# The first modulation as small products on TensorE, with products of ones around them, and the Fourier branch split into even and odd tokens

## The chip, the cores and the metric

The kernel runs on one core of a Trainium2 chip. The metric is the device time of one execution in microseconds (us). A core has a matrix engine (TensorE, PE in the profile; its weight loads are listed apart as PEld), three other compute engines (VectorE or DVE, ScalarE or ACT, GpSimd or POOL) and a queue that issues the transfers from memory (SyncE or SP). Each engine works through its own list in order and waits on the others by semaphores.

## The reference

Two layers of a transformer over 256 latent and 256 context tokens of 1024 features. Only what the change touches is shown in full.

```python
m = silu(cond) @ w_mod + b_mod                     # 9 x 1024 values a layer, for latent and context each
u = rms_norm(x, g) * (1 + scale) + shift           # shift, scale: parts 0 and 1 of m for the first sublayer
x = x + 0.5 * gate * (silu(u @ Wa) * (u @ Wb)) @ Wout        # first FFN, 2816 wide
...
# token mixing: attention beside a Fourier branch of 4 groups of 128 channels
f = u @ w_four_in                                  # 512 channels
y = Re(fft2(f.reshape(S, 4, 128), axes=(tokens, channels), norm="ortho"))
merged = sigmoid(ga) * a + sigmoid(gf) * (y @ w_four_out)
...
# second FFN; in layer 1 the context stream is dropped after its keys and values; final RMS norm
```

## The kernel before, in words

Features lie on the 128 partitions; the 512 tokens (256 latent, then 256 context) lie along the free dimension, so `x` is 8 chunks of 128 features by 512 tokens. Every large product is done in three: operands are split into a high part (fp32r) and the remainder, and `mm3` (L369) adds high x high, high x low and low x high (L373, L374, L375). Weights come as blocks of 128 x 1024 through the class `Stream`: `load_to` (L165) issues the transfer, `split_pieces` (L172) makes `whi` on ACT (L184) and `wlo` on DVE or POOL (L185), `next` hands a block out and keeps some loads and splits ahead. The order on each engine is the order in which the Python program issues instructions; all waits come from data and from buffers (46 slots of 4 KB a partition, 7 temporaries, 8 PSUM banks of 128 x 512).

**The start (L1095 to L1198).** The first FFN needs `u`, and `u` needs shift and scale, 16 chunks of 128 values for each of the two conditions. Before, each chunk is a dot product on DVE: `mod_dot` (L299, instruction L302) multiplies a 128 x 1024 block of `w_mod` by the condition, which `cond_spread` has put on all partitions, and sums along the row. For each of the 8 feature chunks `j` the loop at L1157 issues two dots for latent and two for context, the scaled `x` (L1132, on POOL or DVE), two small affines on ACT (L1143, L1145), shift and scale on ACT (L1149), the high part (L1150) and the low part on POOL or DVE (L1154). Meanwhile `ffn` (L597) works on the first `START_PAIRS` = 4 column pairs of the FFN at once: 8 PSUM banks, and for each `k` the products of `u[k]` with 8 weight chunks, latent and context apart (256 columns each). These are the rows `pf`. The other 18 pairs follow one by one, over 512 columns (rows `pa` and `pb`, 48 products a pair). From then on the remaining modulation dots (L302) are dealt out two to a weight block (`tick`), beside the products.

**The Fourier branch (L706 to L755).** It lies at the end of the attention, in heads' steps 8, 9 and 10 and in front of the first merged column. The lists `STEPS` and `TAIL` (L56, L61) give the order of the named steps within a head's turn. For each of 4 groups: `fourier_project` makes 128 channels by all tokens (rows `pfc`); `fourier_channels` multiplies each 128 tokens by a 128 x 256 table of cosines and sines over channels (rows `pch`), and splits the result (`ab`, ACT and DVE); `fourier_positions` multiplies by the 256 x 256 tables over tokens (rows `pseq`). `y` is used by the products `pfo` in the merge (L1068). In layer 1 only the latent tokens go through it.

Of the kernel before, what the change touches and what calls it, by code (L numbers as in the profile page):

```python
# [18 lines left out]
P = 128  # L19
# [21 lines left out]
START_PAIRS = 4  # L41
# [85 lines left out]

def constants():
# [14 lines left out]
    rope = np.stack([cos * scale, sin * scale, cos, sin], axis=1).astype(np.float32)  # L143
# [4 lines left out]
    b = 2 * np.pi * ((s[:, None] * s[None, :]) % S) / S  # L148
    sq = np.stack([np.cos(b), -np.sin(b)]) / math.sqrt(S)
    sq = sq.reshape(2, 2, P, S).transpose(2, 1, 0, 3)  # L150
    return rope.reshape(P, 4 * S), ch.astype(np.float32), np.ascontiguousarray(sq.astype(np.float32)).reshape(P, 4 * S)
# [60 lines left out]
def tile_kernel(ctx: ExitStack, tc, d, out):  # L212
# [45 lines left out]

    def cond_load():
        for n in range(2):  # L260
            cond["row", n] = slot.tile([P, D], F32, tag="s", name="crow")
            nc.sync.dma_start(cond["row", n][:1], d["cond"][n:n + 1, :])

    def cond_spread():

        for n in range(2):
            row = cond.pop(("row", n))
            cond[n] = slot.tile([P, D], F32, tag="s", name="cond")
            for h in range(2):
                hc = slice(h * 512, (h + 1) * 512)  # L270
                ps = bank("pcond")
                nc.tensor.matmul(ps, ones[:1, :], row[:1, hc], start=True, stop=True)
                nc.scalar.activation(cond[n][:, hc], ps, AF.Silu)

    nc.gpsimd.memset(ones, 1.0)
    nc.gpsimd.memset(eps, EPS)
    cond_load()
    nc.sync.dma_start(x[:, :, :S], d["x"][:, :, :S])

# [9 lines left out]
    mod_n = [0, 0, 0]  # L289
# [307 lines left out]
    def ffn(l, f, ss, u, later, after):  # L597
# [8 lines left out]
        if l == 0 and f == 1:  # L606
            for n in range(2):
                cond[n] = slot.tile([P, D], F32, tag="s", name="cond")
                nc.sync.dma_start(cond[n], d["cond"][n:n + 1, :].partition_broadcast(P).rearrange("p a b -> p (a b)"))
# [28 lines left out]
        for n, part in enumerate(stagger):  # L638
            c = cols(part)
            ps = [bank("pf") for _ in range(2 * first)]  # L640
            for k in range(KC):
                if n == 0 and (k * 2 * first) % 8 == 0:
                    w.extend(st.tiles(8))
                for sub in [[s] for s in part] if first == START_PAIRS else [part]:
                    cs = slice(0, S + 2) if e else cols(sub)
                    for q in range(2 * first):
                        mm3(ps[q][:, cs], w[k * 2 * first + q], parts(e.v[k] if e else u[k], cs), k == 0 and sub[0] == part[0], k == KC - 1 and sub[-1] == part[-1])
# [28 lines left out]
    def mixing(l, ss, u, later, after):  # L676
# [31 lines left out]
        def fourier_load():  # L708
            dft["raw"] = slot.tile([P, 1024], F32, tag="s", name="ft"), temp("ft2")
            nc.sync.dma_start(dft["raw"][0], d["dft_sq"])  # L710
            nc.sync.dma_start(dft["raw"][1][:, :256], d["dft_ch"])

        def fourier_tables():

            sq, ch = dft.pop("raw")
            dft["sq"] = [slot.tile([P, 1024], F32R, tag="s", name="dft") for _ in range(2)]
            nc.scalar.activation(dft["sq"][0], sq, AF.Copy)
            nc.gpsimd.tensor_tensor(out=dft["sq"][1], in0=sq, in1=dft["sq"][0].bitcast(F32), op=ALU.subtract)
            dft["ch"] = hilo("dch")
            split(dft["ch"], slice(0, 256), ch[:, :256])  # L720

        fo = {}

        def fourier_project(g):
            tiles = st.tiles(8)
            c = cols(ss)
            ps = bank("pfc")
            for k in range(KC):
                mm3(ps[:, c], tiles[k], parts(u[k], c), k == 0, k == KC - 1)
            fo["f", g] = hilo("f")  # L730
            split(fo["f", g], c, ps[:, c])

        def fourier_channels(g):
            f = fo.pop(("f", g))
            for s in ss:
                ps = bank("pch")
                for t in range(2):
                    fc = slice(s * S + t * P, s * S + (t + 1) * P)
                    q = slice(t * 256, (t + 1) * 256)
                    mm3(ps[:, q], parts(f, fc), parts(dft["ch"], slice(0, 256)), True, True)  # L740
                ab = fo[s, g] = hilo("ab")
                split(ab, slice(0, 512), ps)

        def fourier_positions(g):
            ps = bank("pseq")
            for s in ss:
                ab = fo.pop((s, g))
                for n in range(4):
                    t, cs = divmod(n, 2)
                    q = slice(t * 256 + cs * P, t * 256 + (cs + 1) * P)  # L750
                    rhs = slice(n * S, (n + 1) * S)
                    mm3(ps[:, cols([s])], parts(ab, q), (dft["sq"][0][:, rhs], dft["sq"][1][:, rhs]), n == 0, n == 3)
            c = cols(ss)
# [251 lines left out]
        def fourier(h):  # L1005
            if h == NH:
                fourier_tables()
            if h >= NH:
                fourier_project(h - NH)
# [251 lines left out]
```

## Time and profile before

| | |
|---|---|
| median of 3 runs (lowest, highest) | 2031.62 us (2031.35, 2031.69) |
| the profiled execution, whole | 2031.67 us |
| its span, first to last instruction | 2029.9 us |
| PE, DVE, ACT, POOL busy, share of the span | 98%, 61%, 41%, 40% |
| mean granted TensorE clock | 0.999 of full speed |
| read from memory | 286.91 MB |

A busy share counts an instruction from its start to its end, and products on PE overlap, so the pace of PE is read from the distance between the starts of neighbouring products, not from their durations. "Idle before <- releaser" is the time an engine stood still before a group, and what ended it. The time of the profiled execution lies 1.8 us above its span.

### The profile page before, as it was taken

What the parts mean: (1) busy time and instruction counts of PE and PEld (TensorE: products, weight loads), DVE (VectorE), ACT (ScalarE), POOL (GpSimd) and SP (SyncE); (2) the same over time, 40 slices, a digit from 0 to 9 for tenths busy, and PEclk for the clock granted to TensorE, in tenths of its full rate; (3) what the DMA queues carried; (4) which work ended last, traced back from release to release, by engine and by line L of the source; (5) the groups of instructions that cost most, each with busy time, mean ns of one, the idle gap of its engine ahead of it and who ended that gap; (6) DMA issues with size and microseconds to landing.
All of it is one profiled execution on the core that took longest, in us unless ns stands there. A gap on an engine that the chain in (4) does not pass through costs nothing.

```text
span 2029.9 us, 27251 instructions
## 1 busy us (share of the span) xinstructions
PE 1992.1 (98%) x10476; PEld 1710.7 (84%) x10476; DVE 1244.3 (61%) x1819; ACT 839.2 (41%) x1383; POOL 804.0 (40%) x531
## 2 busy tenths in 40 slices
PE   7899999999999999999999999999999999999998
PEld 5788888888888888988888898888888889998887
DVE  8887787657777234677777543323324687667662
ACT  5532232256666234522322233223323566656661
POOL 7653446445544012244348511111221454214463
PEclk9999999999999999999999999999999999999999
DMA  9355565523332333455559532222421334555461
GB/s 374 119 177 177 177 219 195 168 66 94 105 96 89 94 106 128 149 178 176 157 196 348 181 125 83 83 83 84 129 89 63 116 123 136 170 187 180 154 217 63
DMA packets 86534, 297.08 MB, mean 146 GB/s; under 512 B 9858, under 2 KB 13314, under 8 KB 86404
## 3 DMA queue, kind: packets, MB, share of 16 engines
q1 hardware_dynamic: 86116, 294.82, 43.3%
q8 instruction: 82, 1.34, 0.3%
q10 hardware_dynamic: 288, 0.52, 0.1%
q14 instruction: 48, 0.39, 0.1%
HBM read 286.91 MB, written 1.05 MB: 142 GB/s over the span
## 4 chain that ended last, share of the span: by engine, by line
PE 89%; DVE 4%; DMA 2%; issue 2%; ACT 1%; POOL 1%; SPq 0%; DVEq 0%; POOLq 0%; ACTq 0%
PE po L374 7%; PE po L373 7%; PE po L375 7%; PE pb L375 5%; PE pb L374 5%; PE pb L373 5%; PE pa L374 5%; PE pa L375 5%; PE pa L373 5%; PE pg L374 2%; PE pg L375 2%; PE pg L373 2%; PE po L380 2%; PE pb L380 2%; PE pa L380 2%
## 5 line engine op out<-in xcount | busy, mean ns | idle before, releaser
L185 POOL TENSOR_TENSOR wlo<-wraw,whi 128x1024 fp32r<-128x1024 f32 (+1 forms) x154 | 394.0, 2560 | 555.0 <-ACT whi L184 461.8
L184 ACT ACTIVATE whi<-wraw 128x1024 fp32r<-128x1024 f32 (+1 forms) x400 | 397.3, 1032 | 73.3 <-PE po L374 33.9
L185 DVE TENSOR_TENSOR wlo<-wraw,whi 128x1024 fp32r<-128x1024 f32 x246 | 340.4, 1394 | 115.8 <-ACT whi L184 114.3
L302 DVE SCALAR_TENSOR_TENSOR junk<-mraw,cond 128x1024 bf16<-128x1024 f32 x256 | 363.3, 1463 | 0.3
L373 PE MATMUL po<-g,whi 128*128 128x512 f32 (+1 forms) x616 | 223.8, 363 | 0.0
L374 PE MATMUL po<-g,whi 128*128 128x512 f32 (+1 forms) x616 | 223.3, 362 | 0.0
L375 PE MATMUL po<-g,wlo 128*128 128x512 f32 (+1 forms) x616 | 223.3, 362 | 0.0
L317 POOL TENSOR_SCALAR mval<-macc,small 128x2 f32<-128x2 f32 (+1 forms) x88 | 122.4, 1396 | 212.3 <-DVE junk L302 212.1
L629 ACT ACTIVATE g<-gv 128x512 fp32r<-128x512 f32 (+1 forms) x92 | 51.7, 562 | 371.0 <-DVE gv L628 339.1
L375 PE MATMUL pb<-u,wlo 128*128 128x512 f32 x464 | 180.6, 389 | 0.6 <-POOL wlo L185 0.6
L375 PE MATMUL pa<-u,wlo 128*128 128x512 f32 x464 | 180.6, 389 | 0.3 <-POOL wlo L185 0.3
L373 PE MATMUL pa<-u,whi 128*128 128x512 f32 x464 | 180.7, 389 | 0.0
L374 PE MATMUL pa<-u,whi 128*128 128x512 f32 x464 | 180.6, 389 | 0.0
L374 PE MATMUL pb<-u,whi 128*128 128x512 f32 x464 | 180.5, 389 | 0.0
L373 PE MATMUL pb<-u,whi 128*128 128x512 f32 x464 | 180.5, 389 | 0.0
L628 DVE TENSOR_TENSOR gv<-silu,pb 128x512 f32<-128x512 f32 x58 | 39.9, 688 | 182.4 <-PE pb L375 181.6
L462 DVE SCALAR_TENSOR_TENSOR x<-po,mval,x 128x256 f32<-128x256 f32 x73 | 32.7, 479 | 186.8 <-PE po L375 186.8
L373 PEld LDWEIGHTS po<-g,whi 128*128 128x128 f32 x616 | 116.2, 189 | 18.3
L375 PEld LDWEIGHTS po<-g,wlo 128*128 128x128 f32 x616 | 116.2, 189 | 18.1
L374 PEld LDWEIGHTS po<-g,whi 128*128 128x128 f32 x616 | 116.2, 189 | 18.1
L424 POOL TENSOR_TENSOR acc<-acc,sq 128x256 f32<-128x256 f32 (+1 forms) x46 | 54.1, 1175 | 184.2 <-ACT sq L413 184.1
L413 ACT ACTIVATE sq<-x 128x256 f32<-128x256 f32 (+1 forms) x48 | 24.8, 516 | 233.7 <-DVE x L462 203.0
(261 smaller groups left out, 4700.5 us busy)
## 6 DMA issues: line engine op xcount, KB each, us to landing
wraw<-in_ffn_in SPq DMA_DIRECT2D x176, 512.0 KB, 4.2
mraw<-in_w_mod SPq DMA_DIRECT2D x144, 512.0 KB, 3.8
wraw<-in_ffn_out SPq DMA_DIRECT2D x88, 512.0 KB, 4.4
wraw<-in_qk SPq DMA_DIRECT2D x32, 512.0 KB, 3.8
wraw<-in_g SPq DMA_DIRECT2D x32, 512.0 KB, 3.7
wraw<-in_v SPq DMA_DIRECT2D x16, 512.0 KB, 3.7
wraw<-in_attn SPq DMA_DIRECT2D x16, 512.0 KB, 3.5
wraw<-in_wo SPq DMA_DIRECT2D x16, 512.0 KB, 3.6
```

What stands on the lines that cost most here:

```text
L184: nc.scalar.activation(hi[:, c], raw[:, c], AF.Copy)
L185: eng.tensor_tensor(out=lo[:, c], in0=raw[:, c], in1=hi[:, c].bitcast(F32), op=ALU.subtract)
L302: nc.vector.scalar_tensor_tensor(out=tmp.tile([P, D], BF16, tag="t", name="junk"), in0=mod_raw[n], scalar=1.0, in1=cond[s], op0=ALU.mult, ...
L317: eng.tensor_scalar(out=o, in0=v, scalar1=b_mod[:, b:b + 1], scalar2=0.5 if i % 3 == 2 else 1.0, op0=ALU.add, op1=ALU.mult)
L373: nc.tensor.matmul(ps, hi, uh, start=first, stop=False)
L374: nc.tensor.matmul(ps, hi, ul, start=False, stop=False)
L375: nc.tensor.matmul(ps, lo, uh, start=False, stop=last)
L380: nc.tensor.matmul(ps.rearrange("p (a b) -> p a b", a=2), hi, t[:, :, c], start=first, stop=False)
L424: nc.gpsimd.tensor_tensor(out=self.acc[:, c], in0=self.acc[:, c], in1=sq[:, c], op=ALU.add)
L462: nc.vector.scalar_tensor_tensor(out=x[:, m, c], in0=ps[:, c], scalar=mod(l, 3 * i + 2, m, s), in1=x[:, m, c], op0=ALU.mult, op1=ALU.add)
L628: nc.vector.tensor_tensor(out=v[:, c], in0=sl[:, c], in1=pb[:, c], op=ALU.mult)
L629: nc.scalar.activation(g[j][:, 0, c], v[:, c], AF.Copy)
```

## The change

**Start.** The two condition vectors also come transposed (`cond_t`, 128 x 16). `silu` of them is written into a zeroed tile of 8 chunks by 32 columns (`cond_w`, 2 columns used). The first 2048 columns of `w_mod` come untransposed, 1 MB for each `j`. `first_mod(j)` issues 8 plain fp32 products of 256 columns with 32 stationary columns each; product `k` writes the partitions 32t to 32t + 31 of one bank, t = k mod 4, so four strips are summed apart. DVE copies them out, and `first_sum(j)` adds the four strips and turns the result onto the partitions with two fp32 products of 2 columns against `pick`; two small operations on DVE finish shift and scale. `first_u` makes `u` with two DVE operations and one ACT operation per stream. `START_PAIRS` goes from 4 to 3, so 6 banks are held by `pf`; a new function `start` writes the order out by hand: for `k` = 0 and 1 latent and context apart, for `k` = 2 to 7 both at once over 512 columns, with `first_sum(k+1)` after the first 6 products of `k` and `first_mod(k+2)` after the last 12. `busy` issues fp32 products of ones with ones, 128 columns each: 24 at the very start, 6 and 4 later. The spread conditions (`cond`, for the later dots) are loaded last in the start and their `silu` is done on ACT at `k` = 5. The norm's sum of squares is folded to two products a stream.

**Fourier.** Tokens are renumbered on the host, even ones first, then odd ones (rope tables and output too). `fourier_project` now has tokens as the stationary side and the 512 channels along the free dimension, one bank for each 128 tokens. The position step comes first: for a group and a stream, 128 even tokens and 128 odd tokens are each multiplied by one 128 x 256 table (128 positions, cosine and sine); ACT copies the odd half out, DVE adds and subtracts to get positions 0 to 127 and 128 to 255, and the result is split. Two groups are done at once. The channel step is last and makes `y` over all tokens at once. Loads, table splits and the places in the head steps change accordingly.

PE's list from its first product, before:

```order
L272 MATMUL pcond<-crow,ones 128x512 x4
L1121 MATMUL ss<-sq,ones 128x256 x8
L373 MATMUL pf<-u_148,whi 128x256
L374 MATMUL pf<-u_148,whi 128x256
L375 MATMUL pf<-u_148,wlo 128x256
```

and the same place now (`pwarm` and the second `pf` row are products of ones, `pmod` the modulation, `msb` its copy):

```order
L1142 MATMUL pwarm<-ones 128x128 x24
L1183 MATMUL pmod<-mfirst,cond_w 32x256 x8
L1172 MATMUL ss<-sq,ones 128x256 x2
L1193 MATMUL pmod<-pick,msb 128x2 x2
L1142 MATMUL pf<-ones 128x128 x6
L373 MATMUL pf<-u_180,whi 128x256
L374 MATMUL pf<-u_180,whi 128x256
L375 MATMUL pf<-u_180,wlo 128x256
```

The modulation and the norm now stand on PE in front of the first `pf`; the eight sums of squares have become two for the stream that is needed first.

DVE's list in the start, before (from the first dots on; `junk` is the written-out product of a dot, `macc` its sum):

```order
L302 SCALAR_TENSOR_TENSOR junk,macc<-mraw,cond 128x1024 x2
L1132 TENSOR_TENSOR ut<-x,rinv 128x256
L302 SCALAR_TENSOR_TENSOR junk,macc<-mraw,cond 128x1024
L1154 TENSOR_TENSOR u_148<-ut,u_148 128x256
L302 SCALAR_TENSOR_TENSOR junk,macc<-mraw,cond 128x1024
L1132 TENSOR_TENSOR ut<-x,rinv 128x256
L302 SCALAR_TENSOR_TENSOR junk,macc<-mraw,cond 128x1024 x2
```

and now, one turn of `start` (`k` = 3 to 4):

```order
L1200 TENSOR_SCALAR mval<-pmod,small 128x2
L1200 TENSOR_SCALAR mval<-pmod,bm_80,small 128x2
L1207 SCALAR_TENSOR_TENSOR ut<-x,mval,rinv 128x256 x2
L1211 SCALAR_TENSOR_TENSOR u_183<-ut,mval,u_183 128x256 x2
L1185 COPY msb<-pmod 128x256
```

The dots are gone from DVE here; a turn has a copy, two small operations and four of 256 columns, and in some turns the low part of a weight block.

DVE's list at the end of layer 1's heads, before (`f` is the split projection, `ab` the split channel step, `orinv` the norm of a head's output):

```order
L395 TENSOR_TENSOR f_14526<-pfc_14501,f_14526 128x256
L395 TENSOR_TENSOR ab_14536<-pch_14529,ab_14536 128x512
L944 SCALAR_TENSOR_TENSOR orinv_14541<-pav_14464,sub_g_79,orinv_14541 128x256
L395 TENSOR_TENSOR ao_14560<-orinv_14541,ao_14560 128x256
L185 TENSOR_TENSOR wlo_14564<-wraw_14434,whi_14563 128x1024
L395 TENSOR_TENSOR f_14594<-pfc_14569,f_14594 128x256
L395 TENSOR_TENSOR ab_14604<-pch_14597,ab_14604 128x512
```

and now:

```order
L395 TENSOR_TENSOR f_14353<-pfc_14258,f_14353 128x512
L395 TENSOR_TENSOR f_14356<-pfc_14262,f_14356 128x512
L962 SCALAR_TENSOR_TENSOR orinv_14361<-pav_14290,sub_g_79,orinv_14361 128x256
L395 TENSOR_TENSOR ao_14380<-orinv_14361,ao_14380 128x256
L193 TENSOR_TENSOR wlo_14388<-wraw_14325,whi_14387 128x1024
L756 TENSOR_TENSOR ab_14409<-pseq_14391,odd_14398 128x4x64
L757 TENSOR_TENSOR ab_14409<-pseq_14391,odd_14398 128x4x64
L756 TENSOR_TENSOR ab_14412<-pseq_14400,odd_14407 128x4x64
L757 TENSOR_TENSOR ab_14412<-pseq_14400,odd_14407 128x4x64
L764 TENSOR_TENSOR ab_14416<-ab_14409,ab_14415 128x512
L764 TENSOR_TENSOR ab_14419<-ab_14412,ab_14418 128x512
```

Both halves of the tokens are now projected and split before the position step, which has two additions or subtractions a group.

The diff, cut to its core:

```diff
-START_PAIRS = 4
+START_PAIRS = 3
+WARM = 24
+TOKENS = np.arange(S).reshape(P, 2).T.reshape(-1)
...
-    mod_n = [0, 0, 0]
+    mod_n = [2 * KC, 2 * KC, 0]
...
+            if first == START_PAIRS:
+                ps = start(first, w, u)
...
-        def fourier_project(g):
-            tiles = st.tiles(8)
-            ps = bank("pfc")
-            for k in range(KC):
-                mm3(ps[:, c], tiles[k], parts(u[k], c), k == 0, k == KC - 1)
...
+        def fourier_project(ns, ks):
+            for k in ks:
+                if ns[0] == 0 and k % 2 == 0:
+                    hi, lo = st.next()
+                    fw.extend([(hi[:, :512], lo[:, :512]), (hi[:, 512:], lo[:, 512:])])
+                for n in ns:
+                    if k == 0:
+                        fp[n] = bank("pfc")
+                    mm3(fp[n], parts(u[k], slice(n * P, (n + 1) * P)), fw[k], k == 0, k == KC - 1)
...
+        def fourier_positions(s, gs):
+            for g in gs:
+                ps[g] = bank("pseq")
+                for t in range(2):
+                    q = slice(t * 2 * P, (t + 1) * 2 * P)
+                    mm3(ps[g][:, q], parts(fo["f", 2 * s + t], gc), [p[:, q] for p in dft["p"]], True, True)
+                nc.scalar.activation(odd[g], ps[g][:, 2 * P:].rearrange("p (a b) -> p a b", a=4), AF.Copy)
+            for g in gs:
+                nc.vector.tensor_tensor(out=q[:, :, :P // 2], in0=even, in1=odd[g], op=ALU.add)
+                nc.vector.tensor_tensor(out=q[:, :, P // 2:], in0=even, in1=odd[g], op=ALU.subtract)
...
         def fourier_channels(g):
+            for n in range(2):
+                q = slice((4 + n) * P, (5 + n) * P)
+                mm3(ps[:, c], [p[:, q] for p in dft["p"]], (hi[:, n], lo[:, n]), n == 0, n == 1)
...
         def fourier(h):
+            n = h - NH
+            if n in (0, 1):
+                fourier_project((0, 1), range(n * KC // 2, (n + 1) * KC // 2))
+            if n == 2:
+                if CTX in ss:
+                    fourier_project((2,), range(KC))
+                fourier_positions(LAT, range(NG // 2))
...
+    def busy(ps, n):
+        for _ in range(n):
+            nc.tensor.matmul(ps[:, :P], ones, ones, start=True, stop=True)
+    busy(bank("pwarm"), WARM)
...
+    def first_mod(j):
+        ps = bank("pmod")
+        for k in range(KC):
+            t = k % 4
+            nc.tensor.matmul(ps[32 * t:32 * t + 32, :2 * P], cond_w[:, k, :], raw[k // 4][:, t, :], start=k < 4, stop=k >= 4)
+        nc.vector.tensor_copy(sb, ps[:, :2 * P])
+    def first_sum(j):
+        for i in range(2):
+            nc.tensor.matmul(ps[:, q:q + 2], sb[:, i * P:(i + 1) * P], pick[:, :2], start=True, stop=True)
...
+    def start(first, w, u):
+        first_mod(0)
+        first_norm(LAT, sq)
+        first_sum(0)
+        first_u(0, [LAT])
+        weights_to(0)
+        busy(ps[-1], 6)
+        sq = squares(CTX)
+        products(0, [LAT], every)
+        first_mod(1)
+        first_norm(CTX, sq, 4)
+        first_sum(1)
+        first_u(1, [LAT])
+        weights_to(1)
+        first_u(0, [CTX])
+        products(1, [LAT], every)
+        first_mod(2)
+        first_u(1, [CTX])
+        products(0, [CTX], every)
+        first_sum(2)
+        first_u(2, both)
+        weights_to(2)
+        products(1, [CTX], every)
+        first_mod(3)
+        for k in range(2, KC):
+            products(k, both, every[:2])
+            if k + 1 < KC:
+                first_sum(k + 1)
+                first_u(k + 1, both)
+                weights_to(k + 1)
+            if k == 5:
+                nc.scalar.preload_act_table_set(SILU)
+                for n in range(2):
+                    nc.scalar.activation(cond[n], cond[n], AF.Silu)
+            products(k, both, every[2:])
+            if k + 2 < KC:
+                first_mod(k + 2)
```

More of the change, by code (lines that the diff above doesn't have):

```diff
@@ L257, in tile_kernel @@
     cond = {}
+    nc.gpsimd.memset(ones, 1.0)
+    nc.gpsimd.memset(eps, EPS)
+    cond_t = slot.tile([P, KC, 2], F32, tag="s", name="cond_t")
+    nc.sync.dma_start(cond_t, d["cond_t"])
+    for n in range(2):
+        nc.sync.dma_start(x[:, 4 * n:4 * n + 4, :S], d["x"][:, 4 * n:4 * n + 4, :S])
     def cond_load():
         for n in range(2):
[L261 to L267, printed above, removed]
-            cond[n] = slot.tile([P, D], F32, tag="s", name="cond")
[L269 to L278, printed above, removed]
+            cond[n] = slot.tile([P, D], F32, tag="s", name="cond")
+            nc.sync.dma_start(cond[n], d["cond"][n:n + 1, :].partition_broadcast(P).rearrange("p a b -> p (a b)"))
     def mod_tasks():
@@ L606, in ffn @@
         if l == 0 and f == 1:
[L607 to L609 removed]
+            cond_load()
         def gated(j, pa, pb, c):
@@ L639, in ffn @@
             c = cols(part)
-            ps = [bank("pf") for _ in range(2 * first)]
-            for k in range(KC):
+            if first == START_PAIRS:
+                ps = start(first, w, u)
+            else:
+                ps = [bank("pf") for _ in range(2 * first)]
+            for k in range(KC) if first != START_PAIRS else ():
                 if n == 0 and (k * 2 * first) % 8 == 0:
                     w.extend(st.tiles(8))
[L644 to L647, printed above, removed]
+                cs = slice(0, S + 2) if e else c
+                for q in range(2 * first):
+                    mm3(ps[q][:, cs], w[k * 2 * first + q], parts(e.v[k] if e else u[k], cs), k == 0, k == KC - 1)
                 if n == 0 and k == (E_K if e else 4) and later:
@@ L733, in fourier_channels @@
-        def fourier_channels(g):
[L734 to L753, printed above, removed]
+            raw = dft.pop("raw")
@@ new lines, in squares, with first_norm @@
+        nc.scalar.activation(sqs[1], x[:, 4:, c], AF.Square)
+        nc.vector.tensor_tensor(out=sqs[0], in0=sqs[0], in1=sqs[1], op=ALU.add)
+        nc.vector.tensor_tensor(out=sqs[0][:, :2], in0=sqs[0][:, :2], in1=sqs[0][:, 2:], op=ALU.add)
+        return sqs[0]
+    def first_norm(s, sq, n=0):
+        ps = bank("ss")
+        busy(ps, n)
+        c = cols([s])
+        for m in range(2):
+            nc.tensor.matmul(ps[:, c], ones, sq[:, m, :], start=m == 0, stop=m == 1)
+        rinv[s] = rsqrt(ps, D, c, "rinv")
@@ L1236 @@
         "rope": rope,
-        "dft_ch": dft_ch,
-        "dft_sq": dft_sq,
+        "dft": dft,
     }
```

252 lines of the change are left out of this document (133 added, 119 removed).

## The prediction

> **What bounds the kernel now.** I read the page first, then the busy time by stage, then what PE waited for, then the start in order of time.
>
> ```profile
> span 2029.9 us, 27251 instructions
> PE 1992.1 (98%) x10476; PEld 1710.7 (84%) x10476; DVE 1244.3 (61%) x1819; ACT 839.2 (41%) x1383; POOL 804.0 (40%) x531
> ```
>
> By stage (columns: stretch, length, busy us of each engine, granted clock, DMA share, GB/s):
>
> ```profile
> 0.00:20.00 20.00, 14.61 (x25) 7.76 (x25) 11.73 (x12) 9.14 (x15) 8.16 (x13) 1.00 0.87 321
> 20.00:54.00 34.00, 26.12 (x192) 23.70 (x192) 34.00 (x37) 18.74 (x43) 31.24 (x20) 1.00 1.02 406
> 54.00:87.70 33.70, 25.64 (x192) 23.59 (x192) 31.18 (x40) 18.82 (x38) 30.31 (x19) 1.00 0.30 93
> 87.70:2015.00 1927.30, 1919.26 (x10023) 1649.98 (x10022) 1163.56 (x1726) 791.23 (x1285) 731.74 (x478) 1.00 0.43 141
> ```
>
> From 87.7 to 2015 us PE stands still for 8 of 1927 us, so there a product that goes away is time saved. Before 87.7 PE is not the bound: DVE is full, and transfers are full only until 54. Who PE waits for in the start, and what DVE does up to 87.7:
>
> ```profile
> PE pf L374 <- POOL u L1154: 11.4, 7, 1.6
> PE pf L375 <- POOL wlo L185: 3.7, 8, 0.8
> L302 DVE SCALAR_TENSOR_TENSOR junk<-mraw,cond 128x1024 bf16<-128x1024 f32 x32 | 62.1, 1985 | 0.1
> 87.56 0.28 PE L375 MATMUL pf<-u,wlo 128*128 128x256 f32 x1
> 87.68 0.50 PE L373 MATMUL pa<-u,whi 128*128 128x512 f32 x1
> ```
>
> The modulation dots hold DVE for 62 us; the low parts of `u` on POOL come behind them. The first `pa` at 87.7 is the mark for the start.
>
> **PE's pace.** Starts of neighbouring products in a full stretch:
>
> ```profile
> 1214.75 0.28 PE L374 MATMUL pf<-u,whi 128*128 128x256 f32 x1
> ...
> 1217.39 0.28 PE L375 MATMUL pf<-u,wlo 128*128 128x256 f32 x1
> 1217.51 0.40 PE L373 MATMUL pa<-u,whi 128*128 128x512 f32 x1
> ...
> 1221.84 0.39 PE L374 MATMUL pa<-u,whi 128*128 128x512 f32 x1
> ```
>
> 22 steps in 2.64 us: 0.120 us for 256 columns. 19 steps in 4.33 us: 0.228 us for 512.
>
> **Fourier: the sure part.** The groups of before (one of three lines each):
>
> ```profile
> L373 PE MATMUL pseq<-dft,ab 128*128 128x256 f32 x48 | 13.6, 283 | 0.0
> L373 PE MATMUL pch<-dch,f 128*128 128x256 f32 x24 | 6.8, 282 | 0.0
> L373 PE MATMUL pfc<-u,whi 128*128 128x512 f32 x32 | 13.1, 409 | 0.0
> L373 PE MATMUL pfc<-u,whi 128*128 128x256 f32 x32 | 9.3, 291 | 0.0
> ```
>
> That is 144 + 72 products of 256 for positions and channels, a third of them in layer 1. Layer 0: 144 x 0.120 = 17.3 us become 48 x 0.120 (positions) and 24 x 0.228 (channels) = 11.2: 6.1 less. Layer 1: 72 x 0.120 = 8.6 become 48 x 0.120 = 5.8: 2.9 less. Layer 1's projection: 96 x 0.120 = 11.5 becomes 48 x 0.228 = 10.9: 0.6 less; layer 0's stays at 96 of 512. Sum **9.5 us**, all on PE where PE is full. The two additions, the copy and the split of each position step need DVE and ACT, but what reads them (`pch`) stands behind at least a gate projection of 48 x 0.120 = 5.8 us (layer 1) or 24 x 0.228 = 5.5 us (layer 0). The weak spot is layer 1's last head: its sum of squares `pss` now stands behind 12 products (1.4 us) after the head's values, where there were 42.
>
> ```profile
> PE pss L942 <- ACT osq L928: 1.1, 1, 1.1
> 1745.12 0.38 ACT L928 ACTIVATE osq<-pav 128x256 f32<-128x256 f32 x1 [0.45 <-PE pav L375]
> ```
>
> With no cover at all PE waited 1.1 us at an earlier head; 1.4 us of cover is enough if ACT comes at once, as it does here. I take 0, with 2 us as the upper bound for all new waits here.
>
> **The start, by chains.** Transfers, norm and fp32 products:
>
> ```profile
> 0.00:5.00 5.00, 2.73 (x4) 1.19 (x5) 0.00 (x0) 1.88 (x2) 1.15 (x9) 1.00 0.38 111
> 5.00:10.00 5.00, 4.44 (x6) 1.30 (x4) 2.59 (x3) 1.72 (x3) 2.06 (x2) 1.00 1.04 351
> 10.00:15.00 5.00, 3.78 (x8) 2.52 (x8) 4.63 (x5) 2.41 (x3) 2.29 (x1) 1.00 1.03 410
> 11.33 1.06 ACT L1114 ACTIVATE sq<-x 128x1024 f32<-128x1024 f32 x1 [1.26 <-DMA x<-in_x]
> 16.18 3.55 PE L1121 MATMUL ss<-sq,ones 128*128 128x256 f32 x8 [1.24 <-POOL sq L1118]
> 400.66 0.59 PE L430 MATMUL ss<-acc,ones 128*128 128x256 f32 x2
> L430 PE MATMUL ss<-acc,ones x20: 377/377/380, 400.7 to 2020.4; 128*128 128x256 f32 x20
> ```
>
> Delivered by 10 us: 5 x 111 + 5 x 351 KB = 2.3 MB, then 0.41 MB/us. All of `x` (2.2 MB with what goes ahead) had landed at 11.33, when 2.85 MB were through: a load lands about 0.6 MB after its own bytes. In the new order the first modulation block ends at 2.1 MB: 2.7 MB are through at 11.0 us. The second (4.85 MB) comes at 17.7, the eighth (14.3 MB) at 41; both are asked for later, so DMA is not the bound, and the 1 MB of spread conditions behind them delays only blocks needed after 75 us.
>
> An fp32 product leaves two records. Warm, they are 0.59 - 0.377 = 0.213 us apart (0.43 a product of 256 columns); early, 3.55 / 8 = 0.444 (0.89).
>
> **The disputed price: `first_mod`, f.** No row shows products on a quarter of the columns. All four strips at once: two rounds of 0.43, f = 0.85. None beside another: 16 x 0.213 = 3.4. I take **2.1**, midway, which is also what follows if records start in order, as in every timeline here: a strip's second record waits for its first, the next strip's first runs beside it, 9 x 0.213 and one drain (0.377 - 0.213). [...] `first_sum` is four records bounded by a weight load each; 8 fp32 transposes of 128 columns ran at 0.109:
>
> ```profile
> 1715.62 0.87 PE ptr L894 x8
> ```
>
> I take 0.6 us with the small products behind the loads (0.45 to 0.9).
>
> The links on other engines:
>
> ```profile
> 15.04 0.47 ACT L400 ACTIVATE rinv<-ss,eps 128x256 f32<-128x256 f32 x1 [1.35 <-PE ss L1121]
> L446 DVE SCALAR_TENSOR_TENSOR ut<-x,mval,rinv x72: 471/479/1919, 402.2 to 1847.2; 128x256 f32<-128x256 f32 x72
> L1150 ACT ACTIVATE u<-ut x16: 416/418/420, 18.7 to 83.4; 128x256 fp32r<-128x256 f32 x16
> L809 DVE TENSOR_SCALAR rs<-rs,lam x48: 213/214/217, 456.8 to 1736.3; 128x1 f32<-128x1 f32 x48
> L184 ACT ACTIVATE whi<-wraw 128x1024 fp32r<-128x1024 f32 (+1 forms) x400 | 397.3, 1032 | 73.3 <-PE po L374 33.9
> L185 DVE TENSOR_TENSOR wlo<-wraw,whi 128x1024 fp32r<-128x1024 f32 x246 | 340.4, 1394 | 115.8 <-ACT whi L184 114.3
> ```
>
> First turn: `first_mod` 11.0 to 13.1, two norm products to 14.0, logarithm and exponential to 15.0, `first_sum` and two small operations (0.21 each) to 15.1, scaled `x` 15.6, high part 16.1, then on ACT's list the weight block's high part 17.1, on DVE its low part 18.5: the third product waits for that, and 18 x 0.120 end at 20.5. Second turn the same way: `first_mod` 22.6, four products of ones and the norm 24.3, `first_sum` 24.9, `u` 26.4, low part of the block 28.9, products end at 30.2. From here PE has its own work: 2 x 2.1 + 36 x 0.120 + 0.6 = 9.1, to 39.3. Then `k` = 2 to 7: 108 x 0.228 + 5 x 0.6 + 4 x 2.1 = 36.0, to **75.3**.
>
> Is that covered? After `first_sum` the chain to both streams' low parts is about 0.2 + 2 x 0.21 + 0.48 + 0.42 + 2 x 0.48 + hops = 2.7 us; PE has 12 x 0.228 + 2.1 = 4.8. A block split behind it (0.42 + 1.03 + 1.39 more) is just ready. The table load and two `silu` of 1024 columns on ACT at `k` = 5 (some 3.3 us in front of the last `u`) end before that `u` is asked for, by under 1 us; uncovered they cost 3. DVE has some 4 us in a turn of 6.8, so it is no longer the bound.
>
> After 75.3 there is one more pair, 48 x 0.228 = 10.9: before's point is reached at 86.2, against 87.7. **The start gains 1.5 us**; the price f decides its sign, by 8 us for each us.
>
> The clock: a cold PE at 11 us would make the first `first_mod` and norm 3 us longer. The 24 products of ones are put there for that. In this trace the one-row products went 7 us without getting faster:
>
> ```profile
> L272 PE MATMUL pcond<-crow,ones 1*128 1x512 f32 x8 | 7.2, 1072 | 2.3 <-DMA crow<-in_cond 2.3
> ```
>
> The granted clock reads 1.00 throughout and can't tell. [...]
>
> **Sum.** 2031.7 (the profiled execution, 0.05 from the median; 1.8 us of it lie outside the span and stay) - 9.5 - 1.5 = **2020.7 us**.
>
> **Rivals.**
> - *Four strips at once*, f near 1.0: 8 x 1.1 less, some 0.5 given back where PE reaches a block before its low part: 2012.4. For it: the strips share no columns. Against: two records a product, started in order. [...] Chance 0.22.
> - *The strips don't overlap*, f = 3.6 with the drain: 8 x 1.5 = 12 more, 2032.7. The Fourier gain is there and the start takes it back, no change. For it: the only fp32 rows here run one after the other. Chance 0.18.
> - *Slower: every record pays its whole length.* If a small stationary load can't be hidden under the strip before, each of 16 records costs 0.377 us, f = 6.0: 8 x 3.9 = 31 more, 2052. It is slower by 0.2% from f = 4.0 on. Against: PE's loads are hidden everywhere else. Chance 0.06.
> - *New waits in the Fourier part*: `pss` and `pch` reached too early, two or three waits of the kind seen (1.1 to 2.1 us): 5 us back, 2026. For it: DVE has more there. Chance 0.07.
> - *My forecast*: 0.47, its own range 2016 to 2026 (f from 1.6 to 2.6, clock 3).
>
> **How the numbers follow.** About 0.2% (4 us) is what a measurement of this kernel can tell from no change: faster means under 2027.6, slower over 2035.7. Faster: 0.47 + 0.22 + 0.07 + a little of f near 3 = 0.78; the same 0.16; slower 0.06. The range runs from below the four-strip case, 2010, to 2030; it leaves out most of the serial case and the slow one.
>
> **What would show it.** The first `pa` at about 75 us, DVE no longer full in the start, `pmod` records 0.12 to 0.15 us apart on average (2.1 / 16), first `pf` at about 17; `pseq` 24 a line, `pch` 8 of 512 and 8 of 256 columns a line, at the paces above, no wait over 1 us around them. Wrong if `pmod` records are 0.21 or more apart, if PE waits in the start for `u` or for transfers, or if the time between first `pa` and end shrinks by less than 9.5 less the pair's 10.9, that is grows by more than 1.4.

## The result, and the profile of the changed kernel

| | before | after |
|---|---|---|
| median of the runs | 2031.65 us (4 runs, 2031.35 to 2034.51) | **2015.04 us** (4 runs, 2014.15 to 2016.41) |
| profiled execution | 2031.67 us, span 2029.9 | 2016.41 us, span 2014.5 |
| ratio after/before | | 0.9916, 95% interval 0.9899 to 0.9933 |
| forecast | | 2020.7 us, 2010 to 2030 |

The change makes the kernel 16.6 us faster; 11.0 had been forecast. A second set of runs of the same kernel gave 2015.42 (below). One thing must be known to read the profiled execution: some 3 us of it lie in the last FFN, where from about 1840 us on TensorE's products follow each other 1.7% more slowly than in eleven of the fourteen traces. Whether that comes with the execution or with this kernel is not shown: both profiles of the changed kernel have it, but single times of other kernels, of before too, also lie 2 to 3 us higher now and then (the last section).

The page's head, then the busy time by stage (columns: stretch, length, busy us of PE, PEld, DVE, ACT, POOL, granted clock, DMA share, GB/s):

```profile
span 2014.5 us, 26969 instructions
PE 1992.3 (99%) x10388; PEld 1702.2 (84%) x10388; DVE 1211.7 (60%) x1832; ACT 823.0 (41%) x1335; POOL 735.6 (37%) x492
```

```profile
0.00:20.00 20.00, 16.96 (x119) 14.54 (x119) 9.87 (x14) 7.15 (x9) 1.47 (x10) 0.91 0.92 332
20.00:54.00 34.00, 31.71 (x223) 24.08 (x224) 19.01 (x42) 9.86 (x17) 0.00 (x0) 0.95 1.01 402
54.00:67.90 13.90, 13.90 (x77) 10.88 (x76) 9.68 (x19) 8.44 (x11) 2.48 (x1) 1.00 0.67 230
67.90:2000.00 1932.10, 1923.76 (x9930) 1647.50 (x9929) 1169.30 (x1752) 796.23 (x1295) 729.57 (x479) 1.00 0.43 141
```

The start has changed its bound: from 20 to 54 us DVE is busy 19.0 of 34 us where it was busy all 34, and PE 31.7 where it was 26.1. The granted clock reads below 1.00 in the first two stretches. In before it reads 1.00, but in the first stretch that doesn't mean full speed: its trace has no record of the clock before 19.4 us, and its eight fp32 records at 16 us took 3.55 us, 0.444 each, where later ones are 0.213 apart. What PE waits for in the start (total, times, longest), and the mark at which the start ends:

```profile
PE pf L373 <- ACT u L1208: 1.6, 1, 1.6
PE pf L375 <- DVE wlo L193: 1.3, 2, 0.8
PE pf L373 <- ACT whi L192: 1.3, 1, 1.3
...
67.92 0.39 PE L373 MATMUL pa<-u,whi 128*128 128x512 f32 x1
```

The first `pa` comes at 67.9 us; before 87.7, forecast 75.3. The first turn, and one of the later ones, by PE's timeline (start, length, idle time ahead in brackets):

```profile
8.82 1.08 PE L1183 MATMUL pmod<-mfirst,cond_w 128*32 128x256 f32 x16
9.83 1.13 PE L1172 MATMUL ss<-sq,ones 128*128 128x256 f32 x4
10.80 0.50 PE L1193 MATMUL pmod<-pick,msb 128*128 128x2 f32 x4
11.16 1.58 PE L1142 MATMUL pf<-ones 128*128 128x128 f32 x12
14.04 0.39 PE L373 MATMUL pf<-u,whi 128*128 128x256 f32 x1 [1.30 <-ACT whi L192]
14.27 0.28 PE L374 MATMUL pf<-u,whi 128*128 128x256 f32 x1
15.30 0.39 PE L375 MATMUL pf<-u,wlo 128*128 128x256 f32 x1 [0.75 <-DVE wlo L193]
...
17.88 0.41 PE L374 MATMUL pf<-u,whi 128*128 128x256 f32 x1
18.09 0.41 PE L375 MATMUL pf<-u,wlo 128*128 128x256 f32 x1
18.43 1.54 PE L1183 MATMUL pmod<-mfirst,cond_w 128*32 128x256 f32 x16
```

```profile
40.37 0.39 PE L375 MATMUL pf<-u,wlo 128*128 128x512 f32 x1
40.69 1.07 PE L1183 MATMUL pmod<-mfirst,cond_w 128*32 128x256 f32 x16
41.69 0.50 PE L373 MATMUL pf<-u,whi 128*128 128x512 f32 x1
...
43.20 0.50 PE L1193 MATMUL pmod<-pick,msb 128*128 128x2 f32 x4
43.56 0.48 PE L373 MATMUL pf<-u,whi 128*128 128x512 f32 x1
```

A `first_mod` at a granted clock of 1.00 holds PE for 1.07 us. Charged from the pace of the products around it, it costs 41.69 - 40.37 - 0.228 = 1.09 us, against the 2.1 of the forecast. At 18 us the steps between products are 0.21 us, not 0.12. That is half clock, as the granted clock in stretches of 3.41 us says:

```profile
12.61:16.02 3.41, 1.36 (x10) 1.02 (x9) 2.49 (x3) 2.34 (x3) 0.00 (x0) 1.00 1.06 405
16.02:19.44 3.42, 3.42 (x25) 2.74 (x27) 2.28 (x3) 0.00 (x0) 0.00 (x0) 0.50 1.03 408
19.44:22.85 3.41, 2.83 (x28) 2.22 (x20) 0.93 (x4) 0.85 (x2) 0.00 (x0) 1.00 1.02 406
22.85:26.26 3.41, 1.71 (x10) 1.30 (x11) 2.37 (x4) 1.50 (x3) 0.00 (x0) 1.00 1.03 411
26.26:29.68 3.42, 3.42 (x26) 2.39 (x25) 0.59 (x2) 0.51 (x1) 0.00 (x0) 0.50 1.02 407
```

Each stretch in which PE is busy 1.36 or 1.71 us of 3.41 is followed by one at half clock. At full clock their work would have taken half as long, so as an estimate the two cost up to 2 x 1.7 us.

The Fourier groups (one of three lines each) and the waits around layer 0's part:

```profile
L373 PE MATMUL pseq<-dft,f 128*128 128x256 f32 x24 | 7.0, 290 | 0.0
L373 PE MATMUL pfc<-whi,u 128*128 128x512 f32 x48 | 19.5, 407 | 0.2 <-ACT p L860 0.2
```

```profile
PE pav L374 <- DVE al L872: 0.9, 1, 0.9
PE ptr L918 <- DVE p L832: 0.4, 1, 0.4
PE pfc L373 <- ACT p L860: 0.2, 1, 0.2
```

The counts are those of the arithmetic, 24 position products a line and `pch` in 8 products of 512 and 8 of 256 columns. The three waits, 1.5 us, are new. In layer 1 two more are, where `pch` comes to `ab` before it is split:

```profile
PE pch L373 <- ACT ab L761: 0.4, 1, 0.4
PE pch L374 <- DVE ab L764: 0.3, 1, 0.3
```

Against these 0.7 us, a wait of before for `al` (0.3 us) is gone there and the waits of `pk` for `wlo` are 1.8 us, where they were 2.1.

### The profile page after: what moved, and what is told of

Its sections match the earlier page's. It is cut to its first block, busy times and chain, and to the rows that moved or that the text cites. A ratio compares the mean times of both kernels' runs of the same rounds, so it can differ in the third digit from the quotient of the medians.

```text
span 2014.5 us, 26969 instructions
## 1 busy us (share of the span) xinstructions
PE 1992.3 (99%) x10388; PEld 1702.2 (84%) x10388; DVE 1211.7 (60%) x1832; ACT 823.0 (41%) x1335; POOL 735.6 (37%) x492
## 4 chain that ended last, share of the span: by engine, by line
PE 93%; DVE 3%; ACT 2%; issue 1%; POOL 1%; DVEq 0%; POOLq 0%; ACTq 0%
PE po L375 7%; PE po L374 7%; PE po L373 7%; PE pa L373 5%; PE pb L375 5%; PE pa L375 5%; PE pb L373 5%; PE pa L374 5%; PE pb L374 5%; PE pg L373 2%; PE pg L375 2%; PE pg L374 2%; PE po L380 2%; PE pb L380 2%; PE pa L380 2%; PE pv L696 1%
## 5 line engine op out<-in xcount | busy, mean ns | idle before, releaser
L193 POOL TENSOR_TENSOR wlo<-wraw,whi 128x1024 fp32r<-128x1024 f32 x139 | 366.0, 2635 | 605.4 <-ACT whi L192 487.1
L192 ACT ACTIVATE whi<-wraw 128x1024 fp32r<-128x1024 f32 x392 | 395.5, 1049 | 74.8 <-PE po L374 34.1
L193 DVE TENSOR_TENSOR wlo<-wraw,whi 128x1024 fp32r<-128x1024 f32 x253 | 350.3, 1394 | 117.9 <-ACT whi L192 116.3
L302 DVE SCALAR_TENSOR_TENSOR junk<-mraw,cond 128x1024 bf16<-128x1024 f32 x224 | 303.1, 1395 | 1.1 <-DMA mraw<-in_w_mod 1.1
L373 PE MATMUL pa<-u,whi 128*128 128x512 f32 x472 | 183.6, 389 | 0.0
L374 PE MATMUL pa<-u,whi 128*128 128x512 f32 x472 | 183.6, 389 | 0.0
L373 PE MATMUL pb<-u,whi 128*128 128x512 f32 x472 | 183.6, 389 | 0.0
L374 PE MATMUL pb<-u,whi 128*128 128x512 f32 x472 | 183.6, 389 | 0.0
```

The source lines that it names most:

```text
L192: nc.scalar.activation(hi[:, c], raw[:, c], AF.Copy)
L193: eng.tensor_tensor(out=lo[:, c], in0=raw[:, c], in1=hi[:, c].bitcast(F32), op=ALU.subtract)
L302: nc.vector.scalar_tensor_tensor(out=tmp.tile([P, D], BF16, tag="t", name="junk"), in0=mod_raw[n], scalar=1.0, in1=cond[s], op0=ALU.mult, ...
L373: nc.tensor.matmul(ps, hi, uh, start=first, stop=False)
L374: nc.tensor.matmul(ps, hi, ul, start=False, stop=False)
```

## The experiments

All times are medians. The kernel before ran beside each set and gave 2031.3 to 2031.6. "First `pa`" and "from there to the end" are from each kernel's trace; "the changed kernel" is the one above.

**One strip.** What are the four strips worth?

```diff
-            nc.tensor.matmul(ps[32 * t:32 * t + 32, :2 * P], cond_w[:, k, :], raw[k // 4][:, t, :], start=k < 4, stop=k >= 4)
+            nc.tensor.matmul(ps[:32, :2 * P], cond_w[:, k, :], raw[k // 4][:, t, :], start=k == 0, stop=k == KC - 1)
...
```

> All eight products of each first_mod go to one strip of 32 columns, one after the other into the same rows; the sum over strips falls away (32 rows instead of 128). Theory (the four strips run at the same time, which is why first_mod took 1.07 us instead of the forecast 2.1): the 16 records now follow each other at 0.213 us, first_mod takes 3.4 to 3.6 us, 2.4 more, and with eight of them on PE's path the kernel takes 19 us longer than the changed kernel, about 2034 (range +15 to +21). Rival (a product with 32 stationary columns is short by itself, strips or not): first_mod stays near 1.1 and the time within 3 us of the changed kernel's.

It took 2035.05 us (11 runs), 20.0 more than the changed kernel. The first `pa` is at 88.2. One `first_mod` in PE's timeline:

```profile
49.69 3.64 PE L1183 MATMUL pmod<-mfirst,cond_w 128*32 128x256 f32 x16
53.26 0.50 PE L373 MATMUL pf<-u,whi 128*128 128x512 f32 x1
```

3.64 us against 1.07: 2.57 us more, eight times, are 20.6 us, the whole of the difference. With the products one after the other the kernel is slower than before by 0.18% (ratio 1.0018, 1.0010 to 1.0027), although the Fourier part is in it: whether the whole change is worth anything hangs on the strips.

**Two strips.**

```diff
...
+            s = 32 * (k % 2)
+            nc.tensor.matmul(ps[s:s + 32, :2 * P], cond_w[:, k, :], raw[k // 4][:, t, :], start=k < 2, stop=k >= KC - 2)
...
```

> The products of first_mod on two strips of 32 columns instead of four (64 rows are copied and summed). Theory (a strip's records follow each other at 0.214 us and the strips run side by side): 8 records a strip, first_mod takes 0.86 us more than with four strips, 1.9 in all, the kernel 7 us longer than the changed kernel, about 2022 (6 to 8). Rival (two strips share less well, or more than two add nothing): first_mod at 2.7 or more, or at 1.1.

2021.73 us, 6.3 more than the changed kernel on the same chip (2015.42):

```profile
35.43 1.92 PE L1184 MATMUL pmod<-mfirst,cond_w 128*32 128x256 f32 x16
```

So 3.64, 1.92 and 1.07 us with one, two and four strips. The theory holds.

**Pairs.** My forecast of 2.1 rested on records that start in the order of the program. Here both products of a strip stand one behind the other.

```diff
-            t = k % 4
-            nc.tensor.matmul(ps[32 * t:32 * t + 32, :2 * P], cond_w[:, k, :], raw[k // 4][:, t, :], start=k < 4, stop=k >= 4)
+            t = k // 2
+            nc.tensor.matmul(ps[32 * t:32 * t + 32, :2 * P], cond_w[:, k, :], raw[k // 4][:, k % 4, :], start=k % 2 == 0, stop=k % 2 == 1)
```

> The eight products of first_mod in another order over the strips: both of a strip one after the other, then the next strip. The computation is the same but for the order of the sum. Theory A (each strip has a queue of its own and takes its records as they come, whatever the order in the program): first_mod stays at 1.07 us, no change. Theory B (records start in the order of the program, and a record waits only for the one before it on its own strip; then in the changed kernel's order four strips go together, while here four records of a strip follow each other and only the last runs beside the next strip): 13 steps of 0.21 = 2.7 to 2.9 us, eight times 1.7 = 13 to 15 us longer than the changed kernel, about 2029.

2015.45 us, the changed kernel's time, and the same length of a `first_mod`:

```profile
41.60 1.09 PE L1183 MATMUL pmod<-mfirst,cond_w 128*32 128x256 f32 x16
```

The 16 records start four at a time, 0.216 to 0.24 us apart, in both orders; within four the starts lie 0.007 us apart in the changed kernel and 0.013 here, as if the products were handed out one each 0.007 us and each strip then worked through its own. The records don't name their strip, so which four start together is inferred from the times. Theory A holds, and with it falls the order on which my price rested.

**No products of ones.**

```diff
-    busy(bank("pwarm"), WARM)
...
-        busy(ps, n)
...
-        busy(ps[-1], 6)
```

> The 24 products of ones before the first first_mod, the 6 before the first products and the 4 before the second norm are left out; no result uses them. Theory (TensorE gets the full clock only after a stretch in which it was busy nearly all the time): the granted clock reads half until PE is full, at about 30 us, the first three first_mod take 1.5 to 2.1 us, the norm and the first 36 products of 256 columns run at 0.21 us, and the first pa comes 2 to 7 us later, the kernel at 2017 to 2022, likeliest 2019. Rival (the clock rises and falls by itself, or the start waits for transfers, norms and weight blocks anyway): no change within 1 us.

2015.2 us, no change that can be told; the first `pa` is at 68.9 instead of 67.9. The theory's 2 to 7 us did not come. PE is cold at first, as expected:

```profile
8.58 2.27 PE L1181 MATMUL pmod<-mfirst,cond_w 128*32 128x256 f32 x16 [8.58 <-DMA mfirst<-in_w_mod_first]
10.78 2.08 PE L1170 MATMUL ss<-sq,ones 128*128 128x256 f32 x4
```

That is 2.1 us lost in these two groups (2.27 and 2.08 against 1.08 and 1.13). But in the changed kernel the clock falls back at 16 us, so its products there are no faster, and the lead shrinks to 1.0 us. As placed, the ones bring the full pace early (1.08 us for the first `first_mod`, at 8.8 us) but don't hold it (granted clock 0.50 from 16.0 us).

**Gaps filled.** More ones, in the two stretches where PE waited.

```diff
-        busy(ps[-1], 6)
+        busy(ps[-1], 14)
...
-        first_norm(CTX, sq, 4)
+        spare = first_norm(CTX, sq, 4)
         first_sum(1)
+        busy(spare, 10)
```

> 14 products of ones instead of 6 before the first products, and 10 more between the second first_sum and the second block's products, both in stretches where PE waited for whi, wlo and u. Theory (the half-speed spells at 16 to 19.4 us and 26.3 to 29.7 us come from the idle time in the 3.4 us before each): the granted clock stays 1.00 through one or both spells, 18 products of 256 columns there run at 0.12 instead of 0.21, and the first pa comes up to 3.4 us earlier, the kernel 1 to 3.4 us faster than the changed kernel. Rival 1 (the products then reach the low part of the weight block too early and wait for it): the spells go, the time stays. Rival 2 (the spells are not set by PE's idle time): they stay, and the time is up to 2 us longer, as the added products stand in front of real ones.

2010.97 us, 4.1 less than the changed kernel, where 1 to 3.4 had been expected. The first `pa` is at 65.4, 2.5 us earlier, and only this is shown to come from the filling: from there to the end this trace takes 1943.5 us and the changed kernel's 1946.5, which are the 3 us of the last FFN. The same five stretches of clock (the grid lies 1 us earlier here):

```profile
11.59:15.00 3.41, 3.41 (x32) 3.41 (x32) 1.83 (x5) 2.83 (x5) 0.17 (x1) 1.00 1.08 394
15.00:18.41 3.41, 2.88 (x31) 2.37 (x33) 3.27 (x4) 0.45 (x1) 0.00 (x0) 1.00 1.02 404
18.41:21.83 3.42, 3.19 (x30) 2.60 (x23) 1.44 (x5) 0.81 (x2) 0.00 (x0) 1.00 1.03 411
21.83:25.24 3.41, 3.31 (x29) 3.11 (x28) 2.37 (x4) 1.53 (x3) 0.00 (x0) 1.00 1.03 411
25.24:28.65 3.41, 3.41 (x36) 2.69 (x36) 1.46 (x4) 0.72 (x2) 0.00 (x0) 1.00 1.02 407
```

None of the five has less than 2.88 us of work and none falls to half. Products that compute nothing make the kernel faster, since they stand where PE would have waited.

**Gaps filled, no ones at the beginning.** The edit above, without `pwarm`.

> The filled kernel without the 24 products of ones ahead of the first first_mod. Theory (without them PE is cold at 9 us, the first first_mod and norm take 2.7 us longer, but the full clock comes after the first stretch that real products and fillers fill, so that only the first norm is late): the first pa 1 to 2.5 us later than in the filled kernel, about 2012.5. Rival (the early products of ones are what keeps the clock up later on): half clock up to 20 us and again later, 4 us or more slower than the filled kernel. Rival (they are worth nothing): the filled kernel's time.

2012.5 us, first `pa` at 67.0, 1.6 us later than with them. In these two traces, where nothing throws the clock back, the early ones are worth 1.6 us.

**The changed kernel again, and the filled one beside it**, on one chip.

> The changed kernel once more, unaltered, beside the filled kernel on one chip. Theory (half clock comes in steps of 3.41 us whose grid lies anew in each execution, so that the start differs from execution to execution; beside that every kernel has executions that are some 3 us longer in the last FFN): times spread over 2013 to 2018, the median 2014.5 to 2015.5, and the first pa of this profile lies anywhere from 67.5 to 70. Rival (the first profile was one of its kind): all times within 0.5 us of 2013.4, the first profile's time less the 3 us.

> The kernel with the filled gaps once more, on the same chip as the changed kernel. Theory: 2010.9 in all executions but the few that are 3 us longer, 3.5 to 4.5 us under the changed kernel's median. Rival (the first comparison was made over different chips and days): within 1 us of the changed kernel.

2015.42 us (2012.05 to 2017.54) and 2012.2 us (2010.96, 2011.09, 2013.30, 2013.32). The changed kernel spreads, to a little below the 2013 to 2018 expected; its first `pa` came at 67.2 (a little under what I had allowed), with one spell at half clock where the first profile had two. The filled kernel is 3.2 us under it, a little less than the 3.5 expected, and two of its four executions, more than the few expected, were some 2 us longer. Over both sets the medians of eight runs are 2015.3 and 2011.1. By the traces the filling gives 1.8 to 2.5 us of these 4.2 (first `pa` at 65.4 in both of the filled kernel, at 67.2 and 67.9 in those of the changed one). The rest is the last FFN, which is slower in both traces of the changed kernel and in neither of the filled one; that the filling has a part in this is not shown.

**Old Fourier part with the new start**, and **new Fourier part with the old start**: the diff's Fourier hunks undone in the one, and applied alone in the other.

> The new start with the Fourier part as before (tokens in their own order, channels first, 256 columns each, its own places). Theory (the trace's difference by stretches): layer 0 gave 4.4 us and layer 1 3.5, so this kernel is 7.9 us slower than the changed kernel, about 2023 (7 to 9). Rival (the sum of the prediction, 9.5, hidden by something else in the stretch): 9.5 or more. Beside that: if the 1.9% slower pace of PE in the last FFN belongs to the new Fourier part, it is gone here and the difference is only 5 us; if it belongs to the execution, it comes and goes over the runs of one kernel.

> The kernel before with the new Fourier part alone. Theory (the two parts of the change don't touch each other, and the Fourier part gives the 7.7 us by which the trace of the kernel with the old Fourier part was longer from the first pa to the end): 7.7 us under before, 2023.8 (2023 to 2024.5). Rival (the prediction's 9.5): 2022.0. Rival (the old start's order makes it worth less): above 2025.

2021.52 and 2022.91 us. The second is 8.7 under before, where 7.7 was expected; the first is 6.5 over the changed kernel, less than the 7 to 9 expected (the changed kernel's start varies, and its last FFN was slower in its traces). The stages in the traces show it without that (us between starts of first products; layer 0 from the first `po<-g` to the first `po<-mg`, layer 1 on to its own first `po<-mg`):

| | before | new Fourier, old start | old Fourier, new start | changed |
|---|---|---|---|---|
| first `pa` | 87.7 | 88.0 | 68.5 | 67.9 |
| first `pa` to layer 0's `po<-g` | 197.5 | 196.5 | 206.7 | 206.7 |
| layer 0 with the Fourier part | 501.1 | 496.7 | 501.1 | 496.7 |
| layer 1 with the Fourier part | 1024.6 | 1021.1 | 1024.4 | 1021.1 |

The Fourier part gives 4.4 us in layer 0 and 3.3 to 3.5 in layer 1, whichever start it stands with, so in these stages the parts don't touch each other. The 8.7 us of the kernel with the old start are these 4.4 + 3.5 and the 1.0 us by which its stage behind the first `pa` is shorter, less the 0.3 by which its first `pa` is later. The 1.0 us is no work of the Fourier products: one of before's two waits for `wlo` behind the first `pa` doesn't come up in that trace, and the other is shorter. The forecast's 9.5 is in neither.

**Cover moved.** Layer 0 should have given 6.1. Are the three new waits the rest? This edit and the next are made on the filled kernel.

```diff
             if n in (0, 1):
                 fourier_project((0, 1), range(n * KC // 2, (n + 1) * KC // 2))
+            if n == 1 and CTX in ss:
+                fourier_project((2,), range(KC // 2))
...
-                    fourier_project((2,), range(KC))
+                    fourier_project((2,), range(KC // 2, KC))
```

> The kernel with the filled gaps, and in layer 0 half of the third Fourier projection (12 products of 512 columns) moved one head earlier, in front of that head's values, where the trace of the changed kernel showed waits of 0.9, 0.4 and 0.2 us (pav for al, ptr for p, pfc for p). Theory (these waits are the 1.7 us that layer 0's Fourier part gave less than the arithmetic: 4.4 instead of 6.1): they go, and the time is 1.3 us (1 to 1.5) under that of the filled kernel, 2009.7. Rival (the products that leave the next head's place leave a wait of the same size there): the same time as the filled kernel within 0.3 us.

From the first `pa` to the end 1943.4 us against 1943.5 for the filled kernel: no gain, the rival's case. The wait for `al` went, and another came one head later, where 12 products had left:

```profile
PE pss L960 <- ACT osq L946: 0.8, 1, 0.8
PE ptr L918 <- DVE p L832: 0.4, 1, 0.4
PE pfc L373 <- ACT p L860: 0.2, 1, 0.2
```

**Cover spread.** The fourth projection is halved as well, so that no head loses more than it can spare.

```diff
+                    fourier_project((3,), range(KC // 2))
...
-            fourier_project((3,), range(KC))
+            fourier_project((3,), range(KC // 2, KC))
```

> The filled kernel with layer 0's third and fourth Fourier projections in halves over three places: 12 products more before the values of head 6, 12 before those of the last head instead of 24, 12 after them instead of 24. Theory (the waits at these places need about 1.5 us of cover each, and 12 products of 512 columns are 2.7 us): all three waits (0.9, 0.4 and 0.2 us, or the 0.8 for osq that came in their place) go, 1.4 us under the filled kernel, 2009.5. Rival (what PE waits for there is a chain over ACT and DVE that ends at the same time whatever PE does in between): the waits add up to 1.2 us or more again, the time stays.

From the first `pa` to the end 1942.4 us, 1.1 to 1.2 less, where 1.4 had been expected; the median is 2010.17, ratio to before 0.9898 (0.9884 to 0.9913), the lowest of all. In the stretch from 560 to 800 us two waits are left:

```profile
PE ptr L918 <- DVE p L832: 0.4, 1, 0.4
PE pfc L373 <- ACT p L860: 0.2, 1, 0.2
```

The large wait goes when every place keeps its cover. The two small ones stay, against what I expected: none of the three arrangements removed them.

## Why the prediction was right, and what was off

**Sign and mechanism.** The start changed its bound from DVE to PE, as forecast, and the Fourier part saved what the products say. The gain was 16.6 us where 11.0 was forecast. The difference lies in the sizes of terms, and part of the fit is luck. The forecast's own case, 2016 to 2026, misses 2015.0, which lies in the range only because the range reached down to the four-strip rival. With the measured price of `first_mod` the sum would have read 2020.7 - 8 x 1.01 = 2012.6, or 2.4 us too low. The same working gives 2019.4 for two strips and 2033.2 for one, which measured 2021.73 and 2035.05: too low by 2.3 and 1.9, so the price itself is settled. The 2 us that remain are a balance of errors both ways: the start's first block was earlier and the extra pair cheaper than forecast, the half clock was in no term, the Fourier part gave less, and in the profiled execution the last FFN was slower.

Two of the signs of being wrong need a word. PE did wait for `u` in the start, 1.6 us, once, in the second turn, where the forecast's own chain has a wait for `u` (24.9 to 26.4). And the time from the first `pa` to the end grew from 1942.2 to 1946.5 us, by 4.3, over the limit of 1.4; without the slower last FFN, as in the trace without products of ones (1943.5), it grew by 1.3, just under.

**The step that was off is the price of `first_mod`**, f = 2.1, "what follows if records start in order". It is 1.09. The rival "four strips at once", with f near 1.0, was right on this. One, two and four strips and the order by pairs show it: a strip's second record does wait for its first, at 0.216 us, but nothing on another strip waits with it. The tell-tale forecast for 2.1, records 0.12 to 0.15 us apart on average, was not met: 1.07 / 16 = 0.067. The lower of my two bounds, two rounds of 0.43, was the better row, as it only supposed that the strips are independent; the midpoint had an order of starts in it that no row showed.

**The chain of the start**, mark by mark. `first_mod(0)` began at 8.8 instead of 11.0: its block landed at least 2.2 us earlier than "0.6 MB after its own bytes" (without the ones PE waited for it, to 8.6). The ends of the first two turns, 20.5 and 30.2, were 18.4 and 28.3: the same lead, since what the shorter `first_mod` gave there the half clock took. Then 39.3 became 35.9, with two `first_mod` of 1.7 and 1.1 in place of 2.1 each. The last stretch, forecast at 36.0 us, took 32.0: four `first_mod` at 1.0 us less. Together 2.2 - 0.3 + 1.5 + 4.0 = 7.4 us, the distance from 75.3 to 67.9. In the last stretch `first_sum` was cheaper too (0.36 us of PE, not 0.6), and the first product behind each fp32 group came some 0.1 us late (43.56 to 43.88 is 0.32 us, where 0.228 is the pace), which gave that back.

**The clock.** I had one risk in the sum, a cold PE at 11 us for 3 us, and the ones as its remedy. Without the ones a cold PE did cost 2.1 us in the first two groups (2.27 and 2.08 us against 1.08 and 1.13), so the remedy worked there; that ones on all rows would free the clock was my assumption, which no row of before showed. What I had not thought of is that the clock falls again, to 0.50, after a thinly filled stretch, at 16 and 26 us, up to 2 x 1.7 us by the estimate above. This was in no term and in no rival. That the filling is what prevents it is shown: all seven traces with the new start and unfilled gaps have such a fall in the start, none of the five with filled gaps has. Each spell is 3.41 us long, or once 6.83, and its moment differs between executions: the first one began at 16.0 us in one profile of the changed kernel and at 17.3 in the other. In the profile above, stretches of 3.41 us in which PE was busy for 1.36 and 1.71 us (40 and 50%), with no gap over 1.6 us, were enough for the fall.

**The extra pair** was put at 10.9 us. The stage from the first `pa` to `po` grew by 9.3. Two waits of before in that stage (0.6 and 0.3 us for `wlo`) are gone. With the steps around them, which were longer too, they had put 1.6 us on top of the pace of 0.228, and this is the whole of the difference.

**The change to 32 columns.** The rows allow 0.1 us at each change from products of 128 stationary columns to those of 32: `pmod` starts 0.32 us after the product before it (40.37 to 40.69), where 0.228 is the pace. This is inside the 1.09.

**Fourier.** Layer 1 gave 3.3 to 3.5 us as forecast (3.5), but partly by luck: the gate projection in front of `pch` wasn't enough cover for all of it (0.7 us of new waits), and 0.6 us of before's waits went at the same time. Layer 0 gave 4.4, not 6.1; "I take 0, with 2 us as the upper bound" for new waits was wrong, and the bound right. I had looked for them at `pss` of layer 1's last head. The largest was in layer 0 (`pav` for `al`, 0.9 us), where 12 `pch` had stood as cover between two heads. Spreading the projections gave back 1.2 us, which makes this shown; some 0.5 us of the 1.7 stay with the two small waits.

**What is in neither sum.** The sum over the traces: start 87.7 to 67.9, 19.8 less; the stage of the pairs 9.3 more; Fourier 7.9 less; that is 18.4 less, and the span shrank by 15.4. The 3 us between them are the slower pace in the last FFN of this execution, which eleven of the fourteen traces, before's among them, don't have.

## What to carry to other kernels

Small-stationary fp32 products belong on separate column strips: a chain of eight cost less than a third on four strips here (1.07 and 1.09 us in the two orders tried, against 3.64). Where PE works in bursts, read the granted clock in windows of 3.41 us and fill thin ones with work that needs nothing (windows filled to 40 and 50% were followed by a clock of 0.50 here, and filling them brought the first `pa` from 67.9 to 65.4 us); ones in front of the first product alone bring little if the next gap throws the clock back (67.9 against 68.9 us). When products go, ask which head's wait they covered, and spread what is left evenly.

## What the runs showed of the hardware

- **Half clock after half-filled windows.** Over the traces, windows on the 3.41 us grid that began at full clock, those at the kernel's very end left out: nine that PE filled to 40 to 50%, and one to 60%, were followed by half clock (in the changed kernel 1.36 and 1.71 us of 3.41, then 0.50); all others, from 52% up, were not (in before 1.78 of 3.41 from 26.2 us, then 1.00). Between 52 and 60% it stays open. For the way back, fullness alone doesn't decide: before's two windows full of one-row products (2.3 to 9.1 us) didn't free the clock (the fp32 records from 11.7 us on were 0.427 us apart), nor did one of the kernel without ones (10.1 to 13.5 us), filled to 99% with `first_mod`, a norm and a sum (the full 2 us from 18 us on started 11 products, 0.18 us each, where 0.12 is the pace).
- **Strips.** 3.64, 1.92 and 1.07 us for 16 records of 256 fp32 columns on one, two and four strips: 1.9 and 3.4 times as fast.
- **A slower last FFN in some executions.** Pace by the number of products started (in brackets) in 20 us, first the changed kernel, then the filled one:

```profile
1880.00:1900.00 20.00, 20.00 (x115) 17.32 (x115) 12.80 (x20) 12.96 (x24) 9.50 (x4) 1.00 0.43 136
```

```profile
1880.00:1900.00 20.00, 20.00 (x117) 17.66 (x116) 12.62 (x21) 12.03 (x24) 9.88 (x4) 1.00 0.38 118
```

  The granted clock reads 1.00 in both. Both profiles of the changed kernel and the one of the order by pairs have it, in the last FFN alone, and no other trace; the times of kernels whose profile hasn't got it show single values 2 to 3 us higher as well (before: 2034.5 beside 2031.5), which may be the same. Its cause stays open; no run was made for it.
